# A decoder layer on one core: ten pairs of feed-forward tiles in Strassen's form for the second product, and the embedding's projection between the plain tiles' thirds

## The chip, the cores and the metric

The kernel runs on one core of one Trainium2 chip. The metric is the device time of one execution in microseconds (us), as the median of several runs, lower is better. TensorE is called PE, VectorE DVE, ScalarE ACT, GpSimd POOL, and SyncE SP. SP issues nearly all the DMAs, in order.

## The reference

One decoder layer on 1024 prompt tokens and 8 sample tokens, all in float32. What matters for the change is its last part:

```python
def decoder_layer(x, p, attn_fn, conv_hist, ...):
    h = rms_norm(x, norm_mix_pre)
    q, k, v, u, gates = jnp.split(h @ w_in, IN_SPLITS, axis=-1)
    ...  # attention, convolution branch, merge
    x = x + rms_norm(mix, norm_mix_post)
    h2 = rms_norm(x, norm_ffn_pre)
    gg, uu = jnp.split(h2 @ w_ffn_in, 2, axis=-1)        # 1024 -> 2 x 2816
    f = (jax.nn.silu(gg) * uu) @ w_ffn_out               # 2816 -> 1024
    x = x + rms_norm(f, norm_ffn_post)
    x = x + jax.nn.sigmoid(rms_norm(x, ple_norm) @ w_ple_gate) * (p @ w_ple_proj)
    return x, kv_bufs, conv_tail                         # gate 1024 -> 1024, projection 256 -> 1024
```

Cached keys and values and the convolution's state are also copied to outputs.

## The kernel before

All activations are held transposed: features on the 128 partitions, the T = 1032 tokens along the free axis. A float32 product is made of three matmuls on rounded parts (`mm3`, lines 288 to 290: high x high, low x high, high x low); L120 is the wrapper through which all instructions of the other engines are recorded, so they are told apart by their tiles. The stages follow each other: input projection with attention and convolution, merge and output projection, feed-forward, per-layer embedding.

A scheduler places each engine's instructions from the order in which the code records them and from its own costs and buffers, so code order is not execution order; the parts of the order shown below are the built programs. Generators advanced by `next(...)` and norm chains advanced by `tick(us)` mix later work into earlier stages. Activations of 128 x 1032 live in 43 slots (`act`), raw weights in 3 (`raw`), smaller scratch in 4 (`sc`) and 6 (`rl`) slots. A load whose slot is taken holds SP, and every DMA behind it.

**Start.** During the first projection, SP loads `raw` weights; `strow`, two loads of the convolution's cached state, is transposed by PE (L494, 4 and then 12 matmuls). Cache copies from DRAM to DRAM (`copies`) are handed out one at a time by the loops of the first stages.

**Feed-forward, first product.** There are 22 hidden tiles of 128 features. Tiles 0 to 2 are computed plainly, tiles 3 to 21 in Strassen's form with seven products of 258 columns for each pair of token quarters (`hidden_strassen`). The finished hidden tile is `pk`.

**Feed-forward, second product.** 16 of the tiles, 3 to 18, go through it as 8 pairs in Strassen's form: `pair_sums` makes sums and differences of two tiles' quarters on DVE and writes their high and low parts to DRAM (`d_s`); four groups of two pairs (`PER = 2`) read them back (`mix_hidden`: tiles `ux`, `ush`, `usl`), mix the weights (`mix_weights`: `wx`, `wsh`, `wsl`, on POOL, in the first group partly on DVE), and run seven products per block, 258 columns wide, adding the results to `fa`. The other six tiles, `last = [0, 1, 2, 19, 20, 21]`, are plain: their hidden parts wait in DRAM (`d_h`), come back as `hr`, are split into `uh` and `ul`, and are multiplied in three thirds of 344 columns (`LC`), 18 matmuls for each of 8 output blocks. In the last third the last 4 blocks (`LQ`) run together, tile by tile. After each third, `last_chain` does the two norms and the residual (`res` read back from `d_x`), giving `ph` and `pl`.

**Embedding.** `p_bank` runs 24 matmuls for one output block of `w_ple_gate` in one third; `pg` is scaled by `rbs` on DVE and goes through the sigmoid on ACT. `embed`, two banks later (`LAG = 2`), runs the 6 matmuls of `w_ple_proj` for the same block, multiplies by it from PSUM, adds to `fa` and writes out. `blocks` goes over the gate's tiles in two lots of 4, each through the three thirds.

Of the kernel before, what the change touches and what calls it, by code (L numbers as in the profile page):

```python
# [42 lines left out]
W1 = 6  # L43
W2 = 6
W3 = 4
NPG = 4
MID = 5
WAITS = 2
MT0 = ["m", "O"]
GT0 = ["g", "S0", "g", "S1", "g", "PT"]  # L50
LQ = 4
LAG = 2
TL = 2
TP = 2
PAIRS, PER = 8, 2


@with_exitstack
def decoder_step(ctx: ExitStack, tc: tile.TileContext, ins, outs):
# [360 lines left out]
    for j in range(CLASSIC, NH):  # L420
        wi_st[j] = w_cols(w_ffn_in, j * P)
        w_cols(w_ffn_in, DFF + j * P)
    pairs = [(CLASSIC + 2 * i, CLASSIC + 2 * i + 1) for i in range(PAIRS)]
    last = [j for j in range(NH) if all(j not in x for x in pairs)]
    wi_ff, wi_fs = {}, {}
    for g in range(0, PAIRS, PER):
# [2 lines left out]
                wi_fs[i, half] = w_pair(w_ffn_out, pairs[i], half)  # L429
    for j in last:  # L430
        wi_ff[j] = w_rows(w_ffn_out, j)
    wi_P = [w_cols(w_ple_gate, i * P) for i in range(NPG)]
    wi_pp = [w_rows(w_ple_proj, k) for k in range(2)]
    wi_P += [w_cols(w_ple_gate, i * P) for i in range(NPG, KT)]

# [654 lines left out]
    def triple(i):  # L1090
        for j in range(3):
            for c in (0, 2, 1) if i == 0 and j == 0 else range(3):
                ensure(wi_qkv[i, j] + 1)
                triple_bank(i, j, c)
                attn_slot()
                if c == 1:
                    next(copies, None)
                pump(BUD)
        while attn_busy():
            attn_slot()  # L1100
        done.append(i)
# [70 lines left out]
    for wis, dst in ((wi_gB, d_gB), (wi_gA, d_gA)):  # L1172
        for i in range(KT):
            for c in range(3):
                ensure(wis[i] + 1)
                t0, n = CH[c]
                ps = gemm_bank(wis[i], hs, c)
                s = rl("sg")
                A.activation(s[:, :n], ps[:, :n], AF.Sigmoid)
                SY.dma_start(dst[i, :, t0:t0 + n], s[:, :n])  # L1180
                if attn_busy():
                    attn_slot()
                elif rest:
                    rest.pop()()
                pump(BUD)
        next(copies, None)
    drain_bg()


# [272 lines left out]

    packs = {}

    def pair_sums(i):

        a, b = (packs[j] for j in pairs[i])
        for p in range(2):
# [31 lines left out]
    def hidden_strassen(j, nxt, sums):  # L1500
        pk = packs[j] = act("pk")
        for group in ((0,), (1,)) if j in (CLASSIC, NH - 1) else ((0, 1),):
            quads = []
            for p in group:
                finish(2)
                finish(("t", p))
                quads.append(Quad(j, p, pk))
            for m in ORDER:
                for q in quads:
                    q.product(m)  # L1510
                    q.after(m)
                    tick(1.3)
                    next(nxt, None)
                    next(sums, None)
            if j in last:
                for q in quads:
                    c = slice(q.t0, q.t0 + 2 * QN)
                    SY.dma_start(d_h[j, :, c], pk[:, c])
        del prods[j]

    for js, qs in [(range(2), range(2)), ((2,), (0,)), (range(2), (2,)), ((2,), (1, 2))]:
# [90 lines left out]
    for j in range(CLASSIC, NH):  # L1612
        for _ in prep:
            pass
        prep = prepare(j + 1) if j + 1 < NH else then(mix_weights(0, 0, V), mix_hidden(0, 0))
        hidden_strassen(j, prep, sums)
        for _ in sums:
            pass
        if (j - CLASSIC) % 2 and (j - CLASSIC) // 2 < PAIRS:
            sums = pair_sums((j - CLASSIC) // 2)  # L1620
    for _ in prep:
        pass

# [11 lines left out]
    class OutQuad:  # L1635
# [12 lines left out]
        def product(self, m):  # L1648
# [10 lines left out]
            else:  # L1659
                V.tensor_add(c, c, ps)  # L1660

    G_ = PAIRS // PER
    pre = iter(())
    for g in range(G_):
        if g + 1 < G_:
            ahead = [mix_hidden(g, 1), mix_weights(g + 1, 0), mix_hidden(g + 1, 0), mix_weights(g + 1, 1)]
            if g == 0:
                ahead[0] = then(mix_weights(0, 1, V), ahead[0])
        else:
            ahead = [mix_hidden(g, 1), plain_hidden(last[:1]), plain_hidden(last[1:3]), plain_hidden(last[3:5])]  # L1670
# [9 lines left out]
    for _ in then(pre, plain_hidden(last[5:])):  # L1680
        pass
    wo = [wi_ff[j] for j in last]
    rbs = [None] * 3

    hp = [None] * 3

    def last_chain(ci, sq):
# [14 lines left out]
        r1 = token_rstd(sq2.total(), c)  # L1702
        yield 2
        rb = bcast_cols(r1, c)
        rbs[ci] = sc("rbs")
        A.activation(rbs[ci][:, :n], rb[:, :n], AF.Copy)

    for ci, c in enumerate(LC):
        accs[ci] = SumSq(c)
        nf = KT - LQ if ci == 2 else KT  # L1710
        for f in range(nf):
            ffn_out(last, f, c)
            accs[ci].add(f, fac[f][:, c[0]:c[0] + c[1]])
            tick(2.9)
        if nf < KT:

            t0, n = c
            pss = [bank() for f in range(nf, KT)]
            for k, wi in enumerate(wo):
                (wh, wl), (xh, xl) = W(wi), hid[last[k]]  # L1720
                for f, ps in zip(range(nf, KT), pss):
                    mm3(ps[:, :n], n, wh[:, f], wl[:, f], xh[:, t0:t0 + n], xl[:, t0:t0 + n],
                        k == 0, k == len(wo) - 1)
                tick(TL * LQ / len(wo))
                if k > 1 and k < 5:
                    ensure(wo[-1] + k - 1)
            for f, ps in zip(range(nf, KT), pss):
                fv = fac[f][:, t0:t0 + n]
                V.tensor_add(fv, fv, ps[:, :n])
                accs[ci].add(f, fv)  # L1730
        chains.append([last_chain(ci, accs[ci]), 0, ci])

    pTs = []

    def load_p():
        for k in range(2):
            pin, h, l = act("pin"), act("pTh", F32R), act("pTl", F32R)  # L1740
            SY.dma_start(pin[:, :T], pT_in[k])
            A.activation(h[:, :T], pin[:, :T], AF.Copy)
            V.tensor_sub(l[:, :T], pin[:, :T], h[:, :T].bitcast(F32))
            pTs.append((h, l))

    def p_bank(f, wi, ci):
        c = LC[ci]
        t0, n = c
        finish(ci)
        ps = bank()  # L1750
        sp = W(wi)
# [1 line left out]
            xh, xl = (x[:, k % 3 * n:(k % 3 + 1) * n] for x in hp[ci][k // 3])  # L1753
            mm3(ps[:, :n], n, sp[0][:, k], sp[1][:, k], xh, xl, k == 0, k == KT - 1)
        tick(TP)
        g = rl("pg")
        V.tensor_mul(g[:, :n], ps[:, :n], rbs[ci][:, :n])
        A.activation(g[:, :n], g[:, :n], AF.Sigmoid)
        late.append((f, ci, g))
        if len(late) > LAG:  # L1760
            embed(*late.popleft())

    def embed(f, ci, g):
        t0, n = LC[ci]
        if not pTs:
            load_p()
            ensure(wi_pp[1])
        pp = gemm_bank_rows(wi_pp, f, pTs, LC[ci])
        V.tensor_mul(g[:, :n], g[:, :n], pp[:, :n])
# [97 lines left out]
```

## Time and profile before

| | |
|---|---|
| median of 3 runs | 1680.33 us (1677.91 to 1681.29) |
| profiled execution | 1679.72 us, span 1678.0 us |
| granted clock | 0.999 |
| matmul busy (PE) | 1657.5 us, 99% |
| DVE, ACT, POOL busy | 1206.3, 671.1, 112.5 us |
| DMA | 217 MB, mean 129 GB/s |

The second product's Strassen groups begin at 1321.19 us of the span, and what comes behind the groups begins at about 1488 us.

Reading: a row of a timeline is start, duration, engine, line, operation, output and inputs, and the idle time before with what ended it. A matmul's duration overlaps the next one's, so the pace of a stream is the distance between starts. A row of groups ends with count, busy time, mean ns and the idle time before.

### The profile page before, as it was taken

How to read it: one execution, taken by the hardware profiler on the slowest of the kernel's cores; microseconds unless marked ns; L12 is line 12 of the kernel's file. 1: busy time of each engine (PE TensorE's matmuls, PEld its weight loads, DVE VectorE, ACT ScalarE, POOL GpSimd, SP SyncE). 2: the span in 40 equal slices, each digit the busy share in tenths (PEclk: the TensorE clock that was granted, in tenths of full speed). 3: DMA queues.
4: the chain of work that ended last, by engine and by line, in shares of the span. 5: the costliest groups of instructions: out<-in, count | busy, mean ns of one | idle time of the engine just before them, and what ended most of it. 6: DMA issues, size and time to landing. Idle time of an engine off the chain costs nothing.

```text
span 1678.0 us, 29600 instructions
## 1 busy us (share of the span) xinstructions
PE 1657.5 (99%) x11843; PEld 1630.6 (97%) x11843; DVE 1206.3 (72%) x2156; ACT 671.1 (40%) x1419; POOL 112.5 (7%) x129
## 2 busy tenths in 40 slices
PE   7999999999999999999999999999999999999998
PEld 7999999999999999999999999999999999999998
DVE  7889879859789686744569767766666445668853
ACT  6424444354353245123444444444444431224520
POOL 1000000000000000000000000000000296200000
PEclk9999999999999999999999999999999999999999
DMA  5252322322445264522333244444434676630411
GB/s 199 70 146 84 97 70 73 118 90 84 143 138 195 70 185 128 176 88 67 106 122 102 77 139 140 151 141 144 147 139 152 240 255 243 248 135 14 159 54 45
DMA packets 103296, 217.00 MB, mean 129 GB/s; under 512 B 13074, under 2 KB 64098, under 8 KB 102774
## 3 DMA queue, kind: packets, MB, share of 16 engines
q1 hardware_dynamic: 102966, 214.97, 38.0%
q8 instruction: 93, 1.52, 0.4%
q14 instruction: 45, 0.37, 0.1%
q0 software_dynamic: 192, 0.13, 0.1%
HBM read 157.30 MB, written 71.26 MB: 136 GB/s over the span
## 4 chain that ended last, share of the span: by engine, by line
PE 93%; DVE 2%; DMA 1%; issue 1%; ACT 1%; SPq 0%; POOLq 0%; POOL 0%; DVEq 0%; ACTq 0%
PE g L288 30%; PE g L290 29%; PE g L289 29%; DVE y L120 1%; PE O L690 1%; PE S L645 1%; PE PT L672 1%; DMA strow<-in_state_conv_dram 0%; DMA res<-d_x 0%; DVE wl L120 0%; PE m L347 0%; PE m L335 0%; DMA skv<-d_qkv 0%; PE m L764 0%; DVE acc L120 0%
## 5 line engine op out<-in xcount | busy, mean ns | idle before, releaser
L288 PE MATMUL g<-hh,wh 128*128 128x384 f32 (+1 forms) x1200 | 393.4, 328 | 7.0 <-ACT wh L120 7.0
L290 PE MATMUL g<-hh,wl 128*128 128x384 f32 (+1 forms) x1200 | 384.6, 321 | 0.3 <-DVE wl L120 0.3
L289 PE MATMUL g<-hl,wh 128*128 128x384 f32 (+1 forms) x1200 | 384.8, 321 | 0.0
L120 DVE SCALAR_TENSOR_TENSOR y<-z,taps,y 128x1023 f32<-128x1023 f32 (+14 forms) x240 | 304.0, 1267 | 37.5 <-ACT y L120 31.8
L288 PEld LDWEIGHTS g<-hh,wh 128*128 128x128 f32 x1200 | 226.6, 189 | 14.2 <-ACT wh L120 7.0
L289 PEld LDWEIGHTS g<-hl,wh 128*128 128x128 f32 x1200 | 226.7, 189 | 0.3
L290 PEld LDWEIGHTS g<-hh,wl 128*128 128x128 f32 x1200 | 226.3, 189 | 0.8 <-DVE wl L120 0.8
L120 DVE TENSOR_TENSOR fa<-fa,g 128x258 f32<-128x258 f32 (+1 forms) x216 | 91.4, 433 | 83.9 <-PE g L290 72.7
L120 DVE TENSOR_TENSOR wl<-raw,wh 128x1024 fp32r<-128x1024 f32 x90 | 109.6, 1221 | 31.2 <-ACT wh L120 25.5
L288 PE MATMUL g<-mh,wh 128*128 128x344 f32 x336 | 108.1, 323 | 0.0
L290 PE MATMUL g<-mh,wl 128*128 128x344 f32 x336 | 107.4, 320 | 0.0
L289 PE MATMUL g<-ml,wh 128*128 128x344 f32 x336 | 107.3, 319 | 0.0
L120 ACT ACTIVATE wh<-raw 128x1024 fp32r<-128x1024 f32 x90 | 94.1, 1053 | 17.0 <-issue 7.7
L120 ACT ACTIVATE sg<-g 128x384 f32<-128x384 f32 (+1 forms) x68 | 31.0, 455 | 147.7 <-PE g L290 125.0
L288 PE MATMUL g<-mh,wah 128*128 128x258 f32 x304 | 86.0, 283 | 0.0
L288 PE MATMUL g<-th,wbh 128*128 128x258 f32 x304 | 86.0, 283 | 0.0
L290 PE MATMUL g<-mh,wal 128*128 128x258 f32 x304 | 85.9, 283 | 0.0
L289 PE MATMUL g<-ml,wah 128*128 128x258 f32 x304 | 85.9, 283 | 0.0
L290 PE MATMUL g<-th,wbl 128*128 128x258 f32 x304 | 85.8, 282 | 0.0
L289 PE MATMUL g<-tl,wbh 128*128 128x258 f32 x304 | 85.8, 282 | 0.0
L120 ACT ACTIVATE p<-g 128x258 f32<-128x258 f32 x114 | 43.2, 380 | 82.9 <-PE g L290 82.5
L120 DVE TENSOR_TENSOR acc<-acc,sq 128x344 f32<-128x344 f32 (+2 forms) x123 | 61.3, 513 | 18.0 <-ACT sq L120 15.5
(285 smaller groups left out, 4344.5 us busy)
## 6 DMA issues: line engine op xcount, KB each, us to landing
raw<-in_w_in_dram SPq DMA_DIRECT2D x50, 512.0 KB
raw<-in_w_ffn_in_dram SPq DMA_DIRECT2D x44, 512.0 KB
d_s<-tsh SPq DMA_DIRECT2D x16, 516.0 KB
d_s<-ts SPq DMA_DIRECT2D x16, 516.0 KB
ush<-d_s SPq DMA_DIRECT2D x16, 516.0 KB
usl<-d_s SPq DMA_DIRECT2D x16, 516.0 KB
raw<-in_w_ffn_out_dram SPq DMA_DIRECT2D x32, 256.0 KB
out_kvs_dram<-in_cache_kv_w_dram SPq DMA_DIRECT2D x16, 510.0 KB
```

The lines of the kernel that those rows point to most:

```text
L120: ins = fn(*a, **k)
L288: TE.matmul(ps, hi_w, xh, start=first, stop=False, skip_group_check=more)
L289: TE.matmul(ps, hi_w, xl, start=False, stop=False, skip_group_check=more)
L290: TE.matmul(ps, lo_w, xh, start=False, stop=last, skip_group_check=more)
L645: TE.matmul(sp[h][:, o:o + nk], qT[h * 64:(h + 1) * 64, blk * P:(blk + 1) * P], kT[h * 64:(h + 1) * 64, (blk + 1) * P - nk:(blk + 1) * P], ...
L672: TE.transpose(ps[:, o:o + P], e[:, o:o + P], ident)
L690: TE.matmul(ps[h * 64:(h + 1) * 64, i * P:(i + 1) * P], vtok[:, k0:k0 + 64], self.p[half][:, o:o + P], start=kb == kbs[0], stop=kb == kbs[-1])
```

## The change

1. `PAIRS` goes from 8 to 10: pairs (3,4) to (19,20) and (2,21), in five groups; `last` is `[0, 1]`. Tile 2, computed plainly, is read back from `d_h` as a `pk`. The sums of the ninth pair run beside tile 21, those of the tenth, two steps at a time, in the first group. Tiles 19 to 21 are no longer written to `d_h`.
2. The embedding's projection no longer stands in the gate's banks. Its inputs and weights are loaded in the last group (`embeds`), and its 24 banks run in the order: third 0 of the plain tiles, projection of thirds 0 and 1, third 1 of the plain tiles, projection of third 2, third 2 of the plain tiles. ACT copies each result out of PSUM, SP writes it to a new DRAM scratch (`d_e`), and `p_bank` reads it back. The chain behind a gate bank is then scale, sigmoid, multiply, add (`add_embed`, one bank later). The four-block form of the last third is gone; `rbs` is one tile for the three thirds; the gate's tiles go in lots of 7 and 1.
3. The first of the attention triples hands out no cache copies; the gate loops hand out one for each bank, not one for each of the two loops' ends.

```diff
-LQ = 4
-LAG = 2
-TL = 2
-TP = 2
-PAIRS, PER = 8, 2
+LAG = 1
+TE_, TC = 1.2, 0.15
+TP = 2.2
+WIDE = 7
+PAIRS, PER = 10, 2
...
-    pairs = [(CLASSIC + 2 * i, CLASSIC + 2 * i + 1) for i in range(PAIRS)]
+    pairs = [(CLASSIC + 2 * i, CLASSIC + 2 * i + 1) for i in range(PAIRS - 1)] + [(CLASSIC - 1, NH - 1)]
...
-                if c == 1:
+                if c == 1 and i:
                     next(copies, None)
...
-        next(copies, None)
+            if dst is d_gB or i < 2:
+                next(copies, None)
...
-            if j in last:
-                for q in quads:
-                    c = slice(q.t0, q.t0 + 2 * QN)
-                    SY.dma_start(d_h[j, :, c], pk[:, c])
...
-        if (j - CLASSIC) % 2 and (j - CLASSIC) // 2 < PAIRS:
+        if (j - CLASSIC) % 2:
             sums = pair_sums((j - CLASSIC) // 2)
     for _ in prep:
         pass
+    packs[CLASSIC - 1] = act("pk")
+    SY.dma_start(packs[CLASSIC - 1], d_h[CLASSIC - 1])
...
             if g == 0:
                 ahead[0] = then(mix_weights(0, 1, V), ahead[0])
+                ahead[1] = then(zip(*[pair_sums(PAIRS - 1)] * 2), ahead[1])
         else:
-            ahead = [mix_hidden(g, 1), plain_hidden(last[:1]), plain_hidden(last[1:3]), plain_hidden(last[3:5])]
+            ahead = [mix_hidden(g, 1), plain_hidden(last[:1]), plain_hidden(last[1:]), embeds()]
...
+    def embed(ci, ws):
+        t0, n = c = LC[ci]
+        for f in range(KT):
+            pp = gemm_bank_rows(wi_pp, f, pTs, c)
+            s = rl("pe")
+            A.activation(s[:, :n], pp[:, :n], AF.Copy)
+            SY.dma_start(d_e[f, :, t0:t0 + n], s[:, :n])
+            if f % 4 == 3 and ws:
+                ensure(ws.pop(0))
+            tick(TE_)
+
+    last_plain(0)
+    embed(0, [])
+    embed(1, wi_P[:1])
+    last_plain(1)
+    embed(2, wi_P[1:3])
+    last_plain(2)
...
-        g = rl("pg")
-        V.tensor_mul(g[:, :n], ps[:, :n], rbs[ci][:, :n])
+        g, pe = rl("pg"), sc("pe")
+        SY.dma_start(pe[:, :n], d_e[f, :, t0:t0 + n])
+        V.tensor_mul(g[:, :n], ps[:, :n], rbs[:, t0:t0 + n])
         A.activation(g[:, :n], g[:, :n], AF.Sigmoid)
-        late.append((f, ci, g))
+        late.append((f, ci, g, pe))
         if len(late) > LAG:
-            embed(*late.popleft())
+            add_embed(*late.popleft())
...
-    blocks(wi_P, p_bank, 4)
+    blocks(wi_P, p_bank, WIDE)
```

What moves is shown at three places, in the built programs. The first is SP's queue at the start, around 59 us: `raw` are weight tiles of the first projection, `strow` the convolution's state, `out_kvs_dram` a cache copy. Before:

```order
L120 DMA raw_747<-in_w_in_dram 128x1024
L120 DMA raw_1052<-in_w_in_dram 128x1024
L120 DMA strow_819<-in_state_conv_dram 120x1024
L120 DMA out_cvp_dram<-zrow_814 30x128
L120 DMA out_cvs_dram<-zrow_814 8x128
L120 DMA strow_820<-in_state_conv_dram 120x1024
L120 DMA out_kvs_dram<-in_cache_kv_w_dram 16x4064
L120 DMA oh_896<-in_oh_dram 32x390
```

SP's queue at the same place, now:

```order
L119 DMA raw_748<-in_w_in_dram 128x1024
L119 DMA strow_820<-in_state_conv_dram 120x1024
L119 DMA out_cvp_dram<-zrow_815 30x128
L119 DMA out_cvs_dram<-zrow_815 8x128
L119 DMA strow_821<-in_state_conv_dram 120x1024
L119 DMA raw_1051<-in_w_in_dram 128x1024
L119 DMA oh_897<-in_oh_dram 32x390
```

The second weight tile goes from ahead of both `strow` loads to behind them, and the cache copy is gone from here. On PE, which transposes `strow`, the first four transposes stand four matmuls earlier. Before, on PE:

```order
L290 MATMUL g_923<-hh_115,wl_604 128x384
L288 MATMUL g_923<-hh_117,wh_603 128x384
L494 MATMUL m_823<-ident,strow_819 128x120
L494 MATMUL m_834<-ident,strow_819 128x120
L494 MATMUL m_845<-ident,strow_819 128x120
L494 MATMUL m_883<-ident,strow_819 128x120
L289 MATMUL g_923<-hl_118,wh_603 128x384
```

PE now:

```order
L289 MATMUL g_924<-hl_115,wh_604 128x384
L290 MATMUL g_924<-hh_114,wl_605 128x384
L493 MATMUL m_824<-ident,strow_820 128x120
L493 MATMUL m_835<-ident,strow_820 128x120
L493 MATMUL m_846<-ident,strow_820 128x120
L493 MATMUL m_884<-ident,strow_820 128x120
L288 MATMUL g_924<-hh_116,wh_604 128x384
```

They stood behind the seventh matmul of the 384-wide bank and now stand behind its third.

The second place is SP's queue ahead of the first Strassen group of the second product, around 1310 us. Before:

```order
L120 DMA d_h<-pk_13723 128x516 x2
L120 DMA ux_14101<-d_s 128x774
L120 DMA ux_14102<-d_s 128x774
L120 DMA ush_14104<-d_s 128x1032
L120 DMA usl_14105<-d_s 128x1032
L120 DMA d_h<-pk_13959 128x516
L120 DMA ux_14101<-d_s 128x258
L120 DMA ux_14102<-d_s 128x258
L120 DMA ux_14103<-d_s 128x2x516
L120 DMA ush_14141<-d_s 128x1032
L120 DMA usl_14142<-d_s 128x1032
```

SP's queue ahead of the first group, now:

```order
L119 DMA d_s<-tsh_13987 128x1032
L119 DMA ux_14110<-d_s 128x774
L119 DMA d_s<-ts_13986 128x1032
L119 DMA ux_14111<-d_s 128x774
L119 DMA d_s<-bh_13988 128x774
L119 DMA d_s<-pk_13452 128x258
L119 DMA d_s<-pk_13722 128x516
L119 DMA ush_14113<-d_s 128x1032
L119 DMA usl_14114<-d_s 128x1032
L119 DMA ux_14110<-d_s 128x258
L119 DMA ux_14111<-d_s 128x258
L119 DMA ux_14112<-d_s 128x2x516
```

The group's `ush`, `usl` and the rest of its `ux` now stand behind the last writes of the ninth pair's sums (`d_s<-pk`), which were not there.

The third place is the end of DVE's queue, after the last matmuls; the second input `g` of a `pg` is the projection's bank in PSUM. Before:

```order
L120 TENSOR_TENSOR pg_18147<-g_18122,rbs_17530 128x344
L120 TENSOR_TENSOR pg_18071<-pg_18071,g_18150 128x344
L120 TENSOR_TENSOR fa_14222<-fa_14222,pg_18071 128x344
L120 TENSOR_TENSOR pg_18109<-pg_18109,g_18160 128x344
L120 TENSOR_TENSOR fa_14385<-fa_14385,pg_18109 128x344
L120 TENSOR_TENSOR pg_18147<-pg_18147,g_18170 128x344
L120 TENSOR_TENSOR fa_14387<-fa_14387,pg_18147 128x344
```

The end of DVE's queue now:

```order
L119 TENSOR_TENSOR pg_18488<-pg_18488,pe_18489 128x344
L119 TENSOR_TENSOR fa_14422<-fa_14422,pg_18488 128x344
L119 TENSOR_TENSOR pg_18521<-g_18496,rbs_16939 128x344
L119 TENSOR_TENSOR pg_18521<-pg_18521,pe_18522 128x344
L119 TENSOR_TENSOR fa_14422<-fa_14422,pg_18521 128x344
L119 TENSOR_TENSOR pg_18554<-g_18529,rbs_16939 128x344
L119 TENSOR_TENSOR pg_18554<-pg_18554,pe_18555 128x344
L119 TENSOR_TENSOR fa_14422<-fa_14422,pg_18554 128x344
```

The scaling by `rbs`, which stood several operations ahead of the end, is now the last matmul's first follower.

More of the change, by code (lines that the diff above doesn't have):

```diff
@@ L45 @@
 W3 = 4
-NPG = 4
 MID = 5
@@ L147, in decoder_step @@
     d_s = scratch("d_s", (PAIRS, 2, P, 2, 7 * QN))
+    d_e = scratch("d_e", (KT, P, T))
     d_o = scratch("d_o", (3, 2, P, S))
@@ L431, in decoder_step @@
         wi_ff[j] = w_rows(w_ffn_out, j)
-    wi_P = [w_cols(w_ple_gate, i * P) for i in range(NPG)]
     wi_pp = [w_rows(w_ple_proj, k) for k in range(2)]
-    wi_P += [w_cols(w_ple_gate, i * P) for i in range(NPG, KT)]
+    wi_P = [w_cols(w_ple_gate, i * P) for i in range(KT)]
     xin = {}
@@ L1463, in decoder_step, with pair_sums @@
     packs = {}
-    def pair_sums(i):
+    def pair_sums(i, ps=(0, 1)):
         a, b = (packs[j] for j in pairs[i])
-        for p in range(2):
+        for p in ps:
             t0 = 2 * p * QN
@@ L1660, in product, with embeds @@
                 V.tensor_add(c, c, ps)
+    pTs = []
+    def embeds():
+        for k in range(2):
+            pin, h, l = act("pin"), act("pTh", F32R), act("pTl", F32R)
+            SY.dma_start(pin[:, :T], pT_in[k])
+            yield
+            A.activation(h[:, :T], pin[:, :T], AF.Copy)
+            V.tensor_sub(l[:, :T], pin[:, :T], h[:, :T].bitcast(F32))
+            pTs.append((h, l))
+            yield
+        for wi in wi_pp:
+            ensure(wi)
+            yield
     G_ = PAIRS // PER
@@ L1679, in decoder_step @@
                     next(pre, None)
-    for _ in then(pre, plain_hidden(last[5:])):
+    for _ in pre:
         pass
-    wo = [wi_ff[j] for j in last]
-    rbs = [None] * 3
+    rbs = act("rbs")
     hp = [None] * 3
@@ L1704, in last_chain, with last_plain @@
         rb = bcast_cols(r1, c)
-        rbs[ci] = sc("rbs")
-        A.activation(rbs[ci][:, :n], rb[:, :n], AF.Copy)
-    for ci, c in enumerate(LC):
+        A.activation(rbs[:, t0:t0 + n], rb[:, :n], AF.Copy)
+    def last_plain(ci):
+        c = LC[ci]
         accs[ci] = SumSq(c)
-        nf = KT - LQ if ci == 2 else KT
-        for f in range(nf):
+        for f in range(KT):
             ffn_out(last, f, c)
             accs[ci].add(f, fac[f][:, c[0]:c[0] + c[1]])
[L1714 to L1730, printed above, removed]
-        chains.append([last_chain(ci, accs[ci]), 0, ci])
[L1736 to L1744, printed above, removed]
+            tick(TC)
+        chains.append([last_chain(ci, accs[ci]), 0, ci])
+    def embed(ci, ws):
+        t0, n = c = LC[ci]
+        for f in range(KT):
+            pp = gemm_bank_rows(wi_pp, f, pTs, c)
[11 more added lines that the diff above has]
+    last_plain(2)
     def p_bank(f, wi, ci):
-        c = LC[ci]
-        t0, n = c
+        t0, n = LC[ci]
         finish(ci)
@@ L1755, in p_bank, with add_embed @@
         tick(TP)
-        g = rl("pg")
-        V.tensor_mul(g[:, :n], ps[:, :n], rbs[ci][:, :n])
+        g, pe = rl("pg"), sc("pe")
+        SY.dma_start(pe[:, :n], d_e[f, :, t0:t0 + n])
+        V.tensor_mul(g[:, :n], ps[:, :n], rbs[:, t0:t0 + n])
         A.activation(g[:, :n], g[:, :n], AF.Sigmoid)
-        late.append((f, ci, g))
+        late.append((f, ci, g, pe))
         if len(late) > LAG:
-            embed(*late.popleft())
-    def embed(f, ci, g):
+            add_embed(*late.popleft())
+    def add_embed(f, ci, g, pe):
         t0, n = LC[ci]
[L1765 to L1769, printed above, removed]
+        V.tensor_mul(g[:, :n], g[:, :n], pe[:, :n])
         yv = fac[f][:, t0:t0 + n]
@@ L1774, in decoder_step @@
     late = deque()
-    blocks(wi_P, p_bank, 4)
+    blocks(wi_P, p_bank, WIDE)
     while late:
-        embed(*late.popleft())
+        add_embed(*late.popleft())
 def _t5_bucket(dist):
```

## The prediction

> **What bounds the kernel now.** I read the page first: busy times, then the chain that ended last.
>
> ```profile
> span 1678.0 us, 29600 instructions
> PE 1657.5 (99%) x11843; PEld 1630.6 (97%) x11843; DVE 1206.3 (72%) x2156; ACT 671.1 (40%) x1419; POOL 112.5 (7%) x129
> PE 93%; DVE 2%; DMA 1%; issue 1%; ACT 1%; SPq 0%; POOLq 0%; POOL 0%; DVEq 0%; ACTq 0%
> ```
>
> TensorE (PE) is busy 99% of the span and is 93% of the chain, so time changes in two ways only: by the number and pace of matmuls, and by PE's waits. The waits of PE come next (us in total, times, longest).
>
> ```profile
> PE g L288 <- ACT wh L120: 7.0, 1, 7.0
> PE m L494 <- DMA strow<-in_state_conv_dram: 2.2, 1, 2.2
> PE g L288 <- DVE fa L120: 1.0, 1, 1.0
> PE g L288 <- ACT fa L120: 0.5, 1, 0.5
> ```
>
> The 7.0 us at the program's start is not touched. The second wait and the two on `fa` lie where the change moves work. Then the windows of the stages it touches (length, busy us and count of PE, PEld, DVE, ACT, POOL, then granted clock, DMA share, GB/s): half clock after the strow wait, the stretch before the Strassen groups of the second product, the first of these groups, and everything behind them.
>
> ```profile
> 70.00:73.00 3.00, 3.00 (x12) 3.00 (x13) 0.56 (x1) 0.00 (x0) 0.00 (x0) 0.50 0.03 11
> 1300.00:1320.00 20.00, 20.00 (x170) 20.00 (x169) 9.34 (x23) 5.96 (x14) 0.00 (x0) 1.00 0.68 232
> 1328.00:1340.00 12.00, 10.48 (x83) 9.91 (x82) 3.94 (x8) 2.76 (x8) 5.56 (x8) 1.00 0.92 337
> 1488.00:1674.00 186.00, 183.79 (x1171) 181.76 (x1169) 117.27 (x234) 59.24 (x113) 5.11 (x6) 1.00 0.22 73
> ```
>
> The profiled execution took 1679.72 us, 1.7 more than its span and 0.61 under the median of the runs (1680.33). The sum is made against 1679.72, and 0.6 is added at the end.
>
> **Step 1, tiles against pairs.** A plain tile costs 72 matmuls of 344 columns: the row below has 144 of one pass for six tiles, and there are three passes. Four plain tiles (2, 19, 20, 21) leave the plain part: 4 x 72 = 288 matmuls of 344 go. Two more pairs, by the two programs' instructions, add 336 of 258. Paces are read from starts: 36 steps of 258 columns between the first two rows, 17 of 344 between the last two.
>
> ```profile
> L289 PE MATMUL g<-ul,wh 128*128 128x344 f32 x144 | 46.1, 320 | 0.0
> 1319.74 0.28 PE L288 MATMUL g<-mh,wd 128*128 128x258 f32 x1
> 1324.06 0.28 PE L288 MATMUL g<-ush,wsh 128*128 128x258 f32 x1
> 1670.42 0.32 PE L288 MATMUL g<-pTh,wh 128*128 128x344 f32 x1
> 1673.10 0.32 PE L290 MATMUL g<-pTh,wl 128*128 128x344 f32 x1
> ```
>
> That is 4.32 / 36 = 0.1200 us and 2.68 / 17 = 0.1576 us. Gone: 288 x 0.1576 = 45.4. New: 336 x 0.1200 = 40.3. The exchange is worth -5.1 us, all on the path, since PE has no idle time to lose it in. The saving is small because Strassen's seven products replace eight, and the 0.28 us that a matmul lasts must not be taken for its pace.
>
> [...]
>
> **Step 2, the start.** The convolution's state (`strow`) is transposed by PE at 69.84, 2.21 us late. The rows are PE's and then SP's (which issues all loads), and one load of 516 KB without a crowd, with the instruction that it released.
>
> ```profile
> 66.25 0.34 PE L288 MATMUL g<-hh,wh 128*128 128x384 f32 x1
> 67.30 0.34 PE L288 MATMUL g<-hh,wh 128*128 128x384 f32 x1
> 69.84 1.06 PE L494 MATMUL m<-ident,strow 120*128 120x120 f32 x4 [2.21 <-DMA strow<-in_state_conv_dram]
> 71.04 0.52 PE L290 MATMUL g<-hh,wl 128*128 128x384 f32 x1
> 72.96 0.36 PE L290 MATMUL g<-hh,wl 128*128 128x384 f32 x1
> 73.85 1.40 PE L494 MATMUL m<-ident,strow 120*128 120x120 f32 x12
> 59.01 3.07 SPq L120 DMA_DIRECT2D raw<-in_w_in_dram  x2
> 62.13 0.43 SPq L120 DMA_DIRECT2D strow<-in_state_conv_dram  x1
> 65.23 0.34 SPq L120 DMA_DIRECT2D strow<-in_state_conv_dram  x1
> 1464.70 0.32 SPq L120 DMA_DIRECT2D hr<-d_h  x1
> 1468.35 1.07 ACT L120 ACTIVATE uh<-hr 128x1032 fp32r<-128x1032 f32 x1 [2.94 <-DMA hr<-d_h]
> ```
>
> Matmuls stand (67.30 - 66.25) / 6 = 0.175 us apart before, and (72.96 - 71.04) / 6 = 0.320 behind the wait, at half the granted clock. About nine are slow: 9 x 0.145 = 1.3, so the wait costs 2.2 + 1.3 = 3.5 us. `strow` is late because the second `raw` holds SP until 62.08, when its slot is free. In the new order `strow` follows the first `raw` at once, at about 59.4, and the second `raw` goes behind the second `strow`; one cache copy is no longer issued here. With the 3.65 us of the quoted load (1464.70 to 1468.35) the first `strow` lands at 63 to 64. Its transposes now stand four matmuls earlier, at 66.8: about 3 us of slack. The second leaves at 65.2 as before, lands at 68.9 and is wanted at about 69.4, since what follows moves up with the gain. What is late next is this second one (half a microsecond of slack) and the second `raw`, whose tile is wanted later. Bounds: nothing gained, or all of 3.5. I take -3.0, nearer the upper end, because both landings come out ahead of need.
>
> [...]
>
> The cache copies left out here are issued later, in the gate loop. They are SP's work (0.5 us to issue one) and no engine reads them, so they cost nothing; uncovered, they would delay the next load on SP by one such step.
>
> **Step 3, the first group.** Sums of a new pair (tile 2 and 21) and loads of the first group move. Rows: PE's start of the group's waits, SP's last load for it before, and VectorE's (DVE) subtractions of pair sums.
>
> ```profile
> 1321.19 0.28 PE L288 MATMUL g<-ux,wx 128*128 128x258 f32 x1
> 1330.29 0.39 PE L288 MATMUL g<-ush,wx 128*128 128x258 f32 x1 [1.04 <-DVE fa L120]
> 1314.74 0.38 SPq L120 DMA_DIRECT2D usl<-d_s  x1
> L120 DVE TENSOR_TENSOR ts<-ts,tsh 128x516 fp32r<-128x516 f32 x10 | 6.9, 694 | 8.9 <-ACT tsh L120 8.9
> L120 DVE TENSOR_TENSOR ts<-pk,ts 128x258 f32<-128x258 f32 x8 | 3.4, 420 | 0.0
> ```
>
> Before, the group's last load leaves SP 6.4 us ahead of the group. Now the `ush`, `usl` and `ux` loads stand on SP behind the writes of pair 8's sums, and DVE makes these 97 matmuls (11.6 us) and three subtractions (-1.8) ahead of the group: the loads leave 9.8 us ahead, but all together, with some 3.8 MB counting the writes before them. At the 337 GB/s of the third window they take 11.3 us and land 1.5 us into the group; the first `ush` matmul comes 24 matmuls in (1321.19 to 1324.06) and the second tile's 30, so 3.6 us in: 2 us of slack. At the 232 GB/s of the second window they take 16.4 and land at 6.6: a wait of 3.0, and 1.3 of slow clock as in step 2. Bounds: 0 and +4.3. I take +0.5, near the lower end, because 337 is what this same group drew when it asked for loads in a bunch. On DVE the two extra pairs are four halves, each with four subtractions of 0.42, two of 0.69 and a last 0.42 and 0.69: 4.2 us, 16.8 in all. Two halves fall in tile 21 (20 us, where DVE was 9.3 busy), two in the first group. Covered; if not, the `fa` additions that cost 1.04 us at 1330.29 come later by the excess. The later groups' work on POOL and ACT repeats that of the groups before, at the same load for each.
>
> **Step 4, everything behind the groups.** Rows: DVE's and ACT's groups there, and one load in the chain.
>
> ```profile
> L120 DVE TENSOR_TENSOR wl<-raw,wh 128x1024 fp32r<-128x1024 f32 x11 | 13.2, 1220 | 3.7 <-PE g L289 3.7
> L120 DVE TENSOR_TENSOR pg<-g,rbs 128x344 f32<-128x344 f32 x24 | 12.2, 513 | 31.8 <-PE g L290 31.6 <-ACT rbs L120 0.2
> L120 ACT ACTIVATE rbs<-m 128x344 f32<-128x344 f32 x3 | 1.4, 451 | 3.8 <-PE m L347 3.8
> 1556.14 6.00 DMA res<-d_x
> ```
>
> PE's part there shrinks from 186 to about 186 - 45.4 = 140.6 us, while DVE keeps nearly its 117.3: of the plain tiles one `ul` and three `wl` go (5 us), so 112 of 140, 80% instead of 63%. ACT gains 24 copies of the embedding at 0.451: 10.8, to 70 of 140. SP gains 48 issues (24 writes to `d_e`, 24 loads of it) at 0.3 to 0.5: 14 to 24 us. These 48 transfers of 176 KB are 8.5 MB on top of 73 GB/s x 186 us = 13.6 MB: 157 GB/s in 140 us, under the 337 seen. The embedding's matmuls (6 a bank, 0.95 us) stand where they give the norm chains their time: between thirds, not behind them. Going through DVE's order with the starts of these rows (0.43 to 0.49 for a 344-wide operation, 1.14 for a `wl`), DVE is busy some 97 of the first 102 us, the gate's fourth weight tile is ready 60.6 us into the stage where PE asks for it at 60.7, and the third chunk's second factor at 104.8 for 105.3. So it just holds. Waits there sum to about 186.0 - 183.8 = 2.2 before, and 2.5 by my count after. If a `res` load takes the 6.00 us of the quoted row where its cover is about 4.2, that adds 2. Bounds: -1 (all waits but one hidden) and +4 (each of the two edges above missed by about 2). I take +1.0, between but on the low side, since the hand count closes.
>
> **Step 5, the end.** Rows: the last bank's chain on DVE and ACT.
>
> ```profile
> 1670.62 0.52 DVE L120 TENSOR_TENSOR pg<-g,rbs 128x344 f32<-128x344 f32 x1 [2.64 <-PE g L290]
> 1671.17 0.49 ACT L120 ACTIVATE pg<-pg 128x344 f32<-128x344 f32 x1 [4.23 <-DVE pg L120]
> 1671.63 0.51 DVE L120 TENSOR_TENSOR pg<-pg,g 128x344 f32<-128x344 f32 x1 [0.50 <-PE g L290]
> 1674.13 0.52 DVE L120 TENSOR_TENSOR fa<-fa,pg 128x344 f32<-128x344 f32 x1
> ```
>
> Before, the last matmul is one of the embedding, and a multiplication and an addition follow: 1674.65 - 1673.42 = 1.2 us. Now the last matmul is one of the gate, and scaling, sigmoid, multiplication and addition follow: from 1670.62 to 1671.63, 1.0 us more. +1.0, on the path with nothing beside it.
>
> Sum: -5.1 - 3.0 + 0.5 + 1.0 + 1.0 = -5.6, 1674.1 for such an execution as the profiled one, and 1674.7 for the median.
>
> **The rivals.**
> (A) The other side. Place: SP's queue ahead of the first group. If the bunched loads come at 165 GB/s, they take 23.0 us, land 13.2 into the group, and PE waits 9.6 and loses 1.3 to the clock: 10.9 in place of 0.5, 1685.1. It is slower than before from 176 GB/s down. For it: these loads now share the chip's queues with the weights' and with the pair sums' writes. Against it: 337 and 232 GB/s in the windows. Chance 0.09.
> (B) The last stage gives back more: DVE's order misses both edges, +4 in place of +1 and the first group +1.5 in place of 0.5: 1678.7. For it: 95% of DVE's time and SP's 48 more issues in order, with a load of `d_e` waiting behind its write. Against: the hand count. Chance 0.15.
> (C) The wait for `strow` stays or goes to its second set of transposes: +3.0, 1677.7. For it: half a microsecond of slack at the second. Against: the first leaves SP 2.7 us sooner. Chance 0.11.
> (D) Narrow matmuls do not pay: the exchange is nil from a pace of 45.4 / 336 = 0.135 us for 258 columns, as it could be if the last added groups ran with POOL and DMA at their fullest; then 1679.8. Against: 0.1200 in the quoted rows, on full PE. Chance 0.03. [...]
> The forecast, 1674.7: 0.62.
>
> **How the numbers follow.** A measurement of this kernel tells about 0.2% (3.4 us) from no change: faster is below 1677.0, slower above 1683.7. The forecast alone spans 1671 to 1677.5: step 2 at its full 3.5 and step 4 at -1 give 1672.2, less a microsecond for the paces; step 3 at its far end gives 1678.5. The forecast is faster but for a tenth of it, (B) and (C) are mostly same and in part faster, (D) same, (A) slower, and so is a part where (A), (B) and (C) in milder form add up: faster 0.67, same 0.22, slower 0.11. The range reaches over (B), (C) and (D): 1669.5 to 1681.8.
>
> **What would show it.** Step 1: PE's instructions, +336 and -288, starts 0.120 and 0.158 apart. Step 2: no wait of PE on `strow`, granted clock 1.00 there, a span shorter by 3 up to the first gate. Step 3: waits on DMA for `ush` or `ux` at the first group's start (none, or under a microsecond). Step 4: the stage behind the groups is 140 to 143 us long, PE waits under 3.5 us in it. Step 5: 2.2 us from the last matmul's end to DVE's last. I am wrong if the first group waits for SP, if chain 2 (third chunk) holds the gate's banks, or if `d_e` is waited for.

## The result and the profile after

The changed kernel took 1687.68 us in the median (1685.77 to 1690.83, 6 runs) against 1679.43 us (1677.1 to 1681.29): 1.0052 times as long, interval 1.0038 to 1.0065. The forecast was 1674.7 and faster. The profiled execution is the slowest of the six, 1690.83 us. One execution of experiment 10 below was slow throughout (2691.45 us, granted clock 0.557), and that experiment's ratio is taken without it. The page of the changed kernel:

```profile
span 1689.0 us, 30050 instructions
PE 1658.7 (98%) x11891; PEld 1629.5 (96%) x11891; DVE 1231.2 (73%) x2236; ACT 686.9 (41%) x1463; POOL 143.7 (9%) x161
PE 86%; DVE 6%; DMA 3%; ACT 2%; issue 2%; POOL 1%; SPq 0%; POOLq 0%; DVEq 0%; ACTq 0%
```

PE has the same busy time, but its share of the chain falls from 93% to 86%: the time is in new waits. PE's waits after:

```profile
PE g L288 <- ACT wh L119: 9.1, 2, 7.1
PE m L347 <- POOL r L119: 4.8, 6, 2.0
PE g L288 <- DMA ux<-d_s: 4.2, 2, 2.7
PE g L290 <- DVE wl L119: 2.7, 3, 2.0
PE m L493 <- DMA strow<-in_state_conv_dram: 0.5, 1, 0.5
```

The strow wait has gone from 2.2 to 0.5. New are a second wait on `wh` (9.1 instead of 7.0), 2.7 on `wl`, and 4.2 on the first Strassen group's loads. Where they lie in time is read from PE's starts of the same instruction in both traces: a small product that follows the convolution's transposes, the first matmul behind the gate loops, the first of `th` in the first Strassen product, and the last matmul of the second product's groups. Before:

```profile
80.80 0.38 PE L517 MATMUL m<-oh,tab 32*4 32x130 f32 x2
660.03 0.33 PE L288 MATMUL g<-oh,wh 128*128 128x384 f32 x1
940.52 0.28 PE L288 MATMUL g<-th,wbh 128*128 128x258 f32 x1
1485.56 0.28 PE L290 MATMUL g<-ush,wx 128*128 128x258 f32 x1
```

After:

```profile
78.56 0.38 PE L516 MATMUL m<-oh,tab 32*4 32x130 f32 x2
664.28 0.34 PE L288 MATMUL g<-oh,wh 128*128 128x384 f32 x1
948.24 0.28 PE L288 MATMUL g<-th,wbh 128*128 128x258 f32 x1
1539.29 0.28 PE L290 MATMUL g<-ush,wx 128*128 128x258 f32 x1
```

After less before, the differences are -2.2, +4.25, +7.7 and +53.7, and +11.0 at the end (the spans). Subtracting each from the next gives what each stretch added, in us:

| stretch | by the prediction | measured |
|---|---|---|
| start, to 80 us | -3.0 | -2.2 |
| 80 to 660 us (gate loops) | 0 | +6.5 |
| 660 to 940 us | 0 | +3.5 |
| Strassen groups: 40.3 more matmuls and waits | +40.8 | +46.0 |
| behind them, with the end | -43.4 | -42.7 |

The third row is an accident of this one run. POOL's small power operation, 0.85 to 1.04 us in its other places but the first (1.78), took 4.03 once. PE stood 2.0 us, and the granted clock was 0.54 from 910 to 913 us:

```profile
905.35 4.03 POOL L119 TENSOR_TENSOR r<-r,mhalf 128x3 f32<-128x3 f32 x1 [18.50 <-DVE r L119]
```

None of the twelve experiments' profiles shows it there (0.86 or 0.87 us each). Without its 3.5 the profiled run would be at 1687.3, close to the median. Two places remain.

**The gate loop at 505 us.** PE's, ACT's and DVE's rows of the changed kernel:

```profile
505.19 0.19 PE L848 MATMUL m<-ident,m4x 4*128 4x4 f32 x1 [0.71 <-DVE m4x L119]
507.42 0.69 PE L288 MATMUL g<-hh,wh 128*128 128x384 f32 x1 [2.03 <-ACT wh L119]
511.10 0.69 PE L290 MATMUL g<-hh,wl 128*128 128x384 f32 x1 [2.04 <-DVE wl L119]
504.87 1.28 ACT L119 ACT_TABLE_LOAD   x1
506.16 0.26 ACT L119 ACTIVATE score<-score 128x64 f32<-128x64 f32 x1
506.33 1.99 ACT L119 ACTIVATE wh<-raw 128x1024 fp32r<-128x1024 f32 x2
507.97 1.95 DVE L119 TENSOR_REDUCE sacc<-skv 128x256 f32<-128x1024 f32 x1
509.83 1.22 DVE L119 TENSOR_TENSOR wl<-raw,wh 128x1024 fp32r<-128x1024 f32 x1
```

The sample tokens' attention (`score`, `skv`, `sacc`) runs here piece by piece beside the gate's matmuls. Its two small transposes now stand on PE exactly between two weight tiles, and the next tile's `wh` and `wl` stand in ACT's and DVE's queues behind the attention's exponent (with a table load) and products. In the kernel before, the second transpose stands inside a bank of an earlier weight tile. PE is idle 4.8 us in three pieces and runs at about half pace behind them (0.32 us between matmuls until 514).

**The first Strassen group.** SP's rows of the changed kernel:

```profile
1300.85 13.84 SPq L119 DMA_DIRECT2D raw<-in_w_ffn_out_dram  x3
1317.62 0.32 SPq L119 DMA_DIRECT2D d_s<-ts  x1
1319.83 2.00 SPq L119 DMA_DIRECT2D d_s<-pk  x2
1322.31 0.32 SPq L119 DMA_DIRECT2D ush<-d_s  x1
1333.07 0.89 SPq L119 DMA_DIRECT2D pk<-d_h  x1
1334.02 5.57 SPq L119 DMA_DIRECT2D raw<-in_w_ffn_out_dram  x4
```

Pieces of its chain of waits there (start, length, what):

```profile
1323.18 7.24 DMA ux<-d_s
1334.02 8.26 DMA raw<-in_w_ffn_out_dram
1342.30 7.12 DMA ux<-d_s
```

And the first of PE's waits, at the group's fourth matmul:

```profile
1330.46 0.50 PE L288 MATMUL g<-ux,wx 128*128 128x258 f32 x2 [1.53 <-DMA ux<-d_s]
```

SP stands 13.8 us on `raw` slots for the weight sums, then on the ninth pair's writes, and the first group's `ush` load leaves at 1322.3, 6.1 us ahead of the group (1328.4). PE waits 1.5 us for the `ux` that left behind them at 1323.2, and 0.5 for `usl`. Then the second half's loads stand behind the reload of tile 2 and four more `raw`, leave from 1339.7, and PE waits 0.5 and 2.7 us again. The granted clock is 1.00 behind the first two waits (1331 to 1340 us) and 0.68 behind the longest (1349.4 to 1352.5). The rate is not at fault: 342 to 385 GB/s in 1320 to 1352 us.

### The profile page after: what moved, and what is told of

Same layout as the page of the kernel before. It is cut to its first block, busy times and chain, and to the rows that moved or that the text cites. A ratio compares the mean times of both kernels' runs of the same rounds, so it can differ in the third digit from the quotient of the medians.

```text
span 1689.0 us, 30050 instructions
## 1 busy us (share of the span) xinstructions
PE 1658.7 (98%) x11891; PEld 1629.5 (96%) x11891; DVE 1231.2 (73%) x2236; ACT 686.9 (41%) x1463; POOL 143.7 (9%) x161
## 4 chain that ended last, share of the span: by engine, by line
PE 86%; DVE 6%; DMA 3%; ACT 2%; issue 2%; POOL 1%; SPq 0%; POOLq 0%; DVEq 0%; ACTq 0%
PE g L288 28%; PE g L290 27%; PE g L289 27%; DVE y L119 3%; PE O L689 1%; PE S L644 1%; PE PT L671 1%; DVE acc L119 1%; DMA ux<-d_s 1%; DVE wl L119 1%; POOL r L119 1%; DMA res<-d_x 1%; DMA raw<-in_w_ffn_out_dram 0%; DMA d_e<-pe 0%; PE m L347 0%
## 5 line engine op out<-in xcount | busy, mean ns | idle before, releaser
L119 DVE TENSOR_TENSOR fa<-fa,g 128x258 f32<-128x258 f32 (+1 forms) x272 | 115.3, 431 | 83.1 <-PE g L290 72.0
L119 DVE TENSOR_TENSOR wl<-raw,wh 128x1024 fp32r<-128x1024 f32 x86 | 104.9, 1221 | 45.7 <-ACT wh L119 43.6
L119 ACT ACTIVATE wh<-raw 128x1024 fp32r<-128x1024 f32 x86 | 89.9, 1052 | 13.2 <-issue 7.6
L119 DVE TENSOR_TENSOR pk<-p,g 128x258 f32<-128x258 f32 x76 | 31.3, 421 | 54.9 <-PE g L290 52.0
```

Source lines behind the costliest of these rows:

```text
L119: ins = fn(*a, **k)
```

## The experiments

Ratios are to the kernel before, from runs on the same chip, with their intervals. The changed kernel's is 1.0052 (1.0038 to 1.0065). The kernel before took 1677.66 to 1679.86 us in the sets of runs used here, so two experiments are compared by their ratios, or stretch by stretch in their traces.

**1. Copies in the second gate loop.** In the changed kernel a copy goes out for each weight tile (three banks) of the first gate loop, not for each bank; here the first loop hands out none.

```diff
-            if dst is d_gB or i < 2:
+            if dst is d_gA:
                 next(copies, None)
```

> The changed kernel with one edit: the five cache copies that the first gate loop hands out are handed out by the second gate loop. Theory (the copies in the first loop shift the sample attention's steps so that its two small transposes stand on PE between two weight tiles, and the next tile's wh and wl queue behind its exponent and products): no wait of PE on wh or wl near 505 us, strow gain kept, 6 to 7 us under the changed kernel's 1687.7, so about 1681 (1679.5 to 1682.5). Rival (the stop at 505 us is one run's accident, or follows from the earlier start): about 1687, and a stop of the same size somewhere in the gate loops.

Measured 1686.04 us, 1.0042 (1.0029 to 1.0055). A miss: the waits on `wl` fall to 0.4 and less, but one on `wh` stays at the same place.

```profile
506.60 0.69 PE L288 MATMUL g<-hh,wh 128*128 128x384 f32 x1 [2.75 <-ACT wh L119]
```

In its order the small transposes are inside a bank, but still of the later weight tile, and `wh` stands on ACT behind that bank's sigmoid and a second table load (1.28 us). So the copies inside the loop are not what moves the attention by a tile.

**2. The old copies in the changed kernel.**

```diff
-                if c == 1 and i:
+                if c == 1:
...
-            if dst is d_gB or i < 2:
-                next(copies, None)
+        next(copies, None)
```

> The changed kernel with all three edits of the cache copies undone. Theory: the stop near 505 us goes (-7), the wait on strow comes back (+3): about 1684 (1682 to 1686). Rival (the gate loop's stop is not from the copies): the strow wait alone comes back, about 1690.5.

Measured 1684.1 us, 1.0027 (1.0017 to 1.0036): inside the theory's range, and away from the rival. No wait on `wh` is left at the gate loops, only one of 1.6 us on the attention's `smx`; the strow wait comes back, though at 1.3 us.

**3. The new copies in the kernel before.** The same lines, the other way round.

> The kernel before with the edits of the cache copies alone. Theory: strow wait gone (-3), stop of some 7 us in the first gate loop: about 4 us slower than before, 1683.5 (1682 to 1685.5). Rival: only the start's gain, 1676.5.

Measured 1683.69 us, 1.0020 (1.0011 to 1.0029), with the stop in the gate loop:

```profile
508.00 0.44 PE L288 MATMUL g<-hh,wh 128*128 128x384 f32 x1 [2.03 <-ACT wh L120]
511.67 0.69 PE L290 MATMUL g<-hh,wl 128*128 128x384 f32 x1 [2.42 <-DVE wl L120]
```

The edits of the copies alone make the old kernel slower: its trace gains 1.7 us by 80 us and loses 6.7 in the gate loops.

**4. The copies brought ahead.** The second triple hands out what the first no longer does.

```diff
-                if c == 1 and i:
+                if c == 1 and i or c == 2 and i == 1:
...
-            if dst is d_gB or i < 2:
-                next(copies, None)
+        next(copies, None)
```

> The changed kernel with the first attention triple handing out no cache copies, as changed, but the second triple handing out three more and the gate loops as before, so that 32 copies are ahead of the gate loops' ends as before. Theory (what moved the sample attention by one weight tile is the number of copies issued ahead of it, not the copies inside the gate loop): PE and ACT have the old order at the gate loop, no wait of PE on wh or wl over 1 us there, the strow gain stays: 6 to 7 us under the changed kernel, 1681 (1680 to 1683). Rival (an earlier start always shifts the phase of the gate loop against the sample attention): a wait of 2 to 3 us stays there, 1685 to 1687.

Measured 1681.86 us, 1.0024 (1.0015 to 1.0032). All waits of PE between 485 and 512 us are one:

```profile
490.51 0.27 PE L842 MATMUL m<-ident,smx 128*4 128x128 f32 x1 [0.64 <-DVE smx L119]
```

The old order is back at the gate loop and the strow gain is kept. By the ratios 4.7 us come back, less than the 6 to 7 expected; in the trace the gate loops give back 6.2. Up to this place experiment 1 differs from this one by the three copies alone, since neither has handed out a copy in the gate loop by then. So what shifts the sample attention by a weight tile is how many copies the scheduler has had ahead of it: three fewer put it later. By which rule the scheduler does so was not traced.

**5. The same three copies in the kernel before**, edited as in experiment 4's first line.

> The kernel before with one edit: three cache copies handed out by the second attention triple, not the first. Theory (this is the start's gain alone, since the gate loops keep their old order): no wait of PE on strow over 0.6 us, 2.5 to 3 us under the kernel before, ratio 0.9983 (0.9975 to 0.9993). Rival (the load of the second weight tile, now behind strow, is late for its matmuls and takes it back): ratio 0.9995 to 1.0005.

Measured 1677.78 us, 0.9994 (0.9985 to 1.0003): the profile's span is 1675.5 instead of 1678.0, but by the ratio and the medians it is 1 to 2 us, between theory and rival, and the interval reaches over no change.

**6. Pair sums deferred by a group.**

```diff
-        if (j - CLASSIC) % 2:
+        if (j - CLASSIC) % 2 and (j - CLASSIC) // 2 < PAIRS - 2:
...
-                ahead[1] = then(zip(*[pair_sums(PAIRS - 1)] * 2), ahead[1])
+                ahead[1] = then(zip(*[pair_sums(PAIRS - 2)] * 2), ahead[1])
+            if g == 1:
+                ahead[1] = then(zip(*[late_pair()] * 2), ahead[1])   # reload of tile 2, then its pair's sums
```

> The changed kernel with the ninth pair's sums moved from tile 21 into the first Strassen group and the tenth's (with the reload of tile 2) into the second, so that the first group's loads stand behind no writes. Theory (PE waits in the first group because its ux, ush and usl loads are issued too late and all together): PE's waits on ux and usl in the first group fall from 5.2 us to under 1 for the first half and the whole is 4 to 6 us under the changed kernel, about 1682.5 (1681 to 1684.5). Rival (the bunch only moves: sums and reload now hold SP in the second half of the first group or in the second): 1686 to 1688, with waits of PE on loads 20 to 60 us later.

Measured 1685.26 us, 1.0031 (1.0020 to 1.0042): 2.4 us better by the medians, 3.5 by the ratios, less than the theory's 4 to 6 and better than the rival. No wait on a load is left in the first group, although SP still stands 12.3 us on `raw` slots ahead of the second half's loads (from 1319.6 us); so it is the writes and the reload, and not the `raw` slots alone, that made the loads late. A new wait of PE has come in the second group, on DVE's `fa`. The row of DVE ahead of that `fa`, and the wait:

```profile
1395.96 2.67 DVE L119 TENSOR_TENSOR pk<-pk,bh 128x258 fp32r<-128x258 f32 x2
1399.02 0.39 PE L288 MATMUL g<-ush,wsh 128*128 128x258 f32 x1 [1.88 <-DVE fa L119]
```

**7. Deferred and spread**, on the copies of experiment 4: one step of pair sums between two of weight sums.

```diff
+            if g < 2:
+                ahead[1] = inter(late_sums(g, 0), ahead[1])
+                ahead[3] = inter(late_sums(g, 1), ahead[3])
```

> The kernel with its copies as in copies_ahead, and the ninth pair's sums in the first Strassen group, the tenth's in the second, one step at a time between the weight sums instead of two at a time ahead of them. Theory: no wait on loads in the first group, and the 2.0 us wait on DVE's fa that the bunched sums made in the second group falls under 0.7: 1677 to 1679, 2 us under the kernel before. Rival (DVE's subtractions beside POOL's slow down whatever their order): waits on fa of 1.5 to 2.5 us per group, 1680 to 1682.

Measured 1686.08 us, 1.0047 (1.0034 to 1.0060), 4 us over experiment 4: a miss on the wrong side of both theories. PE waits on DVE nine times:

```profile
PE g L288 <- DVE fa L119: 5.8, 9, 1.6
```

The author's estimate is that pieces spread over the group meet POOL's weight sums more often; how often was not shown. What one meeting cost is measured in experiment 6, where DVE's two `pk<-pk,bh` took 2.67 us at 1395.96, beside two of POOL's `wx` (1395.92 to 1398.08), and 1.03 at 1390.90; experiment 12 has more of them.

**8. Loads ahead of the weight sums.**

```diff
-        prep = prepare(j + 1) if j + 1 < NH else then(mix_weights(0, 0, V), mix_hidden(0, 0))
+        prep = prepare(j + 1) if j + 1 < NH else then(mix_hidden(0, 0), mix_weights(0, 0, V))
...
-                ahead[0] = then(mix_weights(0, 1, V), ahead[0])
+                ahead[0] = then(ahead[0], mix_weights(0, 1, V))
```

> The changed kernel with the first Strassen group's loads recorded ahead of its weight sums (both halves), the pair sums where the change puts them. Theory (the loads are late because SP stands on a raw slot and on the ninth pair's writes): the first half's loads go out ahead of both and PE's waits on ux and usl there are gone, but the weight sums, later now, are waited for (wsl or wsh, 1 to 3 us), and the second half's loads still stand behind the reload of tile 2: 1684 to 1687. Rival (the loads are late because of the rate at which they come, not of their place): no difference, 1687 to 1688.5.

Measured 1683.89 us, 1.0042 (1.0027 to 1.0057); span 1680.8. The ratio's interval overlaps the changed kernel's, so the gain is read from the traces: from the first `th` of the first product to the groups' end it takes 587.5 us, and 591.1 in the changed kernel. The waits on loads are gone from both halves, more than expected; what is waited for in the first group is DVE's and ACT's `fa`, not the weight sums.

**9. The projection back in the gate.**

```diff
-LAG = 1
+LAG = 2
...
-WIDE = 7
+WIDE = 4
...
-    embed(0, [])
-    embed(1, wi_P[:1])
...
-    embed(2, wi_P[1:3])
...
-        V.tensor_mul(g[:, :n], g[:, :n], pe[:, :n])
+        pp = gemm_bank_rows(wi_pp, f, pTs, LC[ci])
+        V.tensor_mul(g[:, :n], g[:, :n], pp[:, :n])
```

> The changed kernel with the projection's banks back among the gate's banks, multiplied from PSUM (no d_e), gate tiles in lots of 4. The number of matmuls is the same. Theory (the projection's 22.7 us of matmuls cover the norm chains, some 20 us of DVE and ACT for a third, that two plain tiles no longer cover): PE waits 7 to 12 us more behind the thirds, 1696 (1693 to 1702). Rival (the round trip through d_e and ACT's copies cost as much as they cover): 1685 to 1689.

Measured 1700.53 us, 1.0137 (1.0123 to 1.0151). PE waits for the norm chain's `ph`, most of it in one 4.1 us piece, and the mean granted clock is 0.992 (0.996 in the changed kernel):

```profile
PE g L288 <- ACT ph L119: 7.6, 5, 4.1
```

So with two plain tiles left, the projection's new place, with the wider lots and the shorter lag that go with it, is worth 13 us. The waits for `ph` say that its matmuls are the cover that the chains need; lots and lag were not tried by themselves.

**10. Both mends in the changed kernel**: experiments 4 and 8.

> The changed kernel with both mends: copies as in copies_ahead, first Strassen group's loads ahead of its weight sums. Theory (the two lost places are independent, and what is left is -5.1 of the exchange, -2.5 of the start, +2.5 behind the groups and +2 of waits in the first group): 3 us under the kernel before, ratio 0.9985 (0.997 to 1.000). Rival (something else costs 3 us more that no wait shows): ratio 1.001 to 1.002.

Measured 1678.7 us, 0.9992 (0.9983 to 1.0001), the fastest form of the change, level with experiment 5 (0.9994) and not told from the kernel before. PE's waits:

```profile
PE m L347 <- POOL r L119: 2.7, 4, 0.9
PE g L288 <- DVE fa L119: 2.5, 2, 1.6
PE g L288 <- ACT fa L119: 1.6, 3, 0.6
PE m L493 <- DMA strow<-in_state_conv_dram: 0.3, 1, 0.3
```

The two lost places account for the loss: 9 us come back by the medians. In the trace the gate loops give back 7.0 us and the Strassen stretch 2.4; with one mend alone (experiments 4 and 8) they gave 6.2 and 3.6, so they are about independent, though the ratios are too wide to show it. Against the kernel before, the trace has -2.2 us at the start, -0.5 in the gate loops, -0.1 up to 940 us, +43.7 in the Strassen stretch (3.4 more than the 40.3 of new matmuls) and -42.6 behind it.

**11. Copies ahead, sums deferred**: experiments 4 and 6.

> The changed kernel with copies as in copies_ahead and the ninth and tenth pairs' sums deferred by a group, two steps at a time, as in sums_deferred. Theory (independent places again): the same as the kernel with the loads first, ratio 0.9985 (0.997 to 1.000), with a wait of 2 us on DVE's fa in the second group. Rival: ratio 1.001 to 1.002.

Measured 1681.26 us, 1.0007 (0.9998 to 1.0015), between theory and rival, with the 1.8 us wait on `fa` in the second group and, in this profile, 1.2 us on strow.

**12. The first weight sums on POOL**, on top of experiment 10.

```diff
-        ... then(mix_hidden(0, 0), mix_weights(0, 0, V))
+        ... then(mix_hidden(0, 0), mix_weights(0, 0))
```

> As the kernel with copies ahead and the loads first, but the first group's first weight sums on POOL, not on DVE, so that DVE has the pair sums alone there. Theory (the waits on DVE's fa in the first group come from DVE doing weight sums and pair sums at once): those waits of 2.4 us fall under 1, ratio 0.997 to 0.999. Rival (POOL, some 15 us for a half group's weights and slowing DVE beside it, becomes what PE waits for at the group's start): waits of PE on wx or wsl of 3 us and more, ratio 1.000 to 1.003.

Measured 1687.26 us, 1.0044 (1.0031 to 1.0058), slower than even the rival, and not by the rival's waits: there is none on `wx` or `wsl`. The wait on `fa` from DVE falls to 0.3, but one on ACT's `fa` of 3.9 us comes later, and PE stands 4.8 us at the group's start for a `p` that DVE has not added. POOL's rows, DVE's beside them, and the wait:

```profile
1317.49 1.46 POOL L119 TENSOR_TENSOR wx<-raw,wx 128x512 fp32r<-128x512 f32 x1
1318.92 1.46 POOL L119 TENSOR_TENSOR wsl<-sa,wsh 128x512 fp32r<-128x512 f32 x1
1320.34 1.44 POOL L119 TENSOR_TENSOR wsl<-sb,wsh 128x512 fp32r<-128x512 f32 x1
1319.16 1.50 DVE L119 TENSOR_TENSOR pk<-pk,bh 128x258 fp32r<-128x258 f32 x1
1320.59 1.48 DVE L119 TENSOR_TENSOR ts<-pk 128x258 f32<-128x258 f32 x1
1322.60 0.41 DVE L119 TENSOR_TENSOR ts<-pk,pk 128x258 f32<-128x258 f32 x1
1324.75 0.58 PE L288 MATMUL g<-mh,wd 128*128 128x258 f32 x1 [4.78 <-DVE p L119]
```

DVE's first two operations here took 1.50 and 1.48 us and ended 0.28 and 0.29 us behind one of POOL's of 1.46 and 1.44; the third, as wide, with POOL at rest, took 0.41. So each of the two ended only behind the POOL instruction beside it; why is not shown.

## Why the prediction was wrong

*Step 1, the exchange (-5.1).* Right. Five groups of 40.3 us each ran at the old pace, 60 us with 502 matmuls in the window 1400 to 1460, and PE has 48 matmuls more in all (11891 against 11843), as 336 - 288. The rival of narrow matmuls that do not pay is out.

*Step 2, the start (-3.0).* Right in kind: the first set of transposes no longer waits, the second, as rival (C) had it in a stronger form, waits 0.5, and the profile gained 2.2 us. The medians of experiment 5 show 1 to 2. The step failed in its last paragraph: "The cache copies left out here ... cost nothing", with "the next load on SP" as the only cover looked at. They cost 6.5 us, not by their transfers but because the built order of the sample attention moved by one weight tile. The prediction read the order at the three places where the code changed, and not where an unchanged stage had been built anew. No rival names this place.

*Step 3, the first group (+0.5, bounds 0 and +4.3).* The size was off, beyond the upper bound: +5.7. The rate was taken right (337 GB/s; 342 and more measured). The departure was wrong: 9.8 us ahead by counting matmuls from DVE's last subtractions, 6.1 in the trace for `ush` and 5.2 for the rest of `ux`. DVE was not late: the write of `ts` left at 1317.6, 10.8 us ahead of the group. But SP then took until 1322.3, 4.7 us, for the other writes and the waits among them, where the count had 1.0. The need was wrong too: 2 us of slack were counted to the first `ush`, 24 matmuls into the group, but PE stopped at the fourth matmul for the `ux` that stands behind `ush` and `usl` in the queue. And the second half's loads, behind the reload of tile 2 and four weight loads, were not costed at all; they were the larger wait, 2.7 and 0.5 against 1.5 and 0.5. Rival (A) had the right place, SP's queue ahead of the group, with the wrong cause (a low rate) and hence too small a chance.

*Step 4, behind the groups (+1.0), and step 5, the end (+1.0).* Right: -42.7 against -43.4 for the stretch. PE's waits there sum to 2.6 us, and PE did not wait for `d_e`. (The groups of the kernel before end at 1485.7 us, not at about 1488; the stage went from 189.0 to 146.8 us, from the groups' last matmul to DVE's last addition.) The end's chain, from the last matmul to the last addition:

```profile
1683.74 0.31 PE L290 MATMUL g<-ph,wl 128*128 128x344 f32 x1
1685.71 0.52 DVE L119 TENSOR_TENSOR fa<-fa,pg 128x344 f32<-128x344 f32 x1
```

That is 2.2 us instead of 1.2. With two plain tiles the stage is as tight as the hand count had it: experiment 9 shows 13 us without the cover.

In sum: -5.1, -2.2 and +2.7 behind the groups (45.4 - 42.7) were near the forecast; with +6.5 in the gate loop and +5.7 in the first group that is +7.6, against a measured +8.25. With both mended the kernel comes to 0.9992, not to the 0.997 of the forecast: the Strassen stretch keeps 3.4 us more than its matmuls, with waits on `fa` of 4.1 us in all against 1.5 before, and the start gives less than 3.

## What to carry to other kernels

When a scheduler builds the program, an edit that only takes DMAs out of one place can move unrelated work elsewhere; compare the built order of every engine at each boundary between weight tiles, not only near the edit, and count a work item that lands between two tiles as a wait for the next tile's conversion (2.03 and 2.04 us here). The loads of the first group were late by their place in the issuing queue (the second half's left from 1339.7 us, behind 5.6 us of `raw` loads), at 342 to 385 GB/s: follow every instruction ahead of it to what that one waits for, for each half of a group, before asking for its rate. In experiment 12 DVE's 258-wide `pk` and `ts` took 1.50 and 1.48 us beside POOL's instructions of 1.46 and 1.44, and another `ts` 0.41 with POOL at rest, so such work is better placed where POOL rests.

## What the runs showed of the hardware

A POOL operation of 0.9 us took 4.0 once in the same program (905 us of the changed kernel's profile), and PE paid 3.5 us for it. DVE was busy without a pause from ahead of its start up to 908.67, and POOL ended 0.7 us behind that. The last row of DVE there:

```profile
907.45 1.22 DVE L119 TENSOR_TENSOR wl<-raw,wh 128x1024 fp32r<-128x1024 f32 x1
```

Why it took so long is not shown: the same operation took 0.87 us at this place in experiments 8 and 9.

DVE's 0.41 us operations took 1.5 beside POOL's of 1.46 in experiment 12. In the kernel before, DVE's 512-wide `wsl` took 1.22 us at most, beside POOL's `sb` of 1.19 and 1.18 (1327 to 1330 us), against 0.69 in the median. Not all of DVE's operations took longer beside POOL: `fa<-fa,g`, with `g` in PSUM, took 0.42 or 0.43 us beside a busy POOL in 1376 to 1400 us of the changed kernel.

The granted clock fell after some short stops and not after others. In the changed kernel it was 0.50 in 511 to 514.2 us behind stops of 0.71, 2.03 and 2.04 us close together, with matmuls 0.32 us apart instead of 0.175, and 0.54 in 910 to 913 us behind a single stop of 1.96; behind 1.53 and 0.54 us in the first Strassen group it stayed at 1.00.
